# An MLP's first strip groups: rectified products written in place, a weight sum moved to GpSimd, and the last output block in two pieces

## The chip, the cores and the metric

The kernel runs on one core of one Trainium2 chip. The metric is the device time of one execution in microseconds (us). Below, PE is TensorE, DVE is VectorE, ACT is ScalarE, POOL is GpSimd and SP is SyncE, which here only issues transfers.

## The reference, cut to what matters

The program is one layer of a flow-matching backbone: attention and DeltaNet branches, an output projection, then an MLP with a squared rectifier. The change touches the MLP alone (D = 1024, FF = 4096; 128 prompt tokens and 512 sample tokens):

```python
def _ffn_sub(x, shift, scale, gate, w_pre, w_post, w1, w2):
    ...
    f = jnp.square(jax.nn.relu(h @ w1)) @ w2
    ...
```

`h` is the normalised and modulated input. The product with `w2` is normalised again, multiplied by a gate and added to `x`.

## The kernel before

**Tiles and precision.** The 640 tokens stand in five tiles of 128: tile 0 is the prompt, tiles 1 to 4 the sample. Every matrix product is made from three: each operand is split into a high part (`whi`, `mhi`, a cast on ACT) and the rest (`wlo`, `mlo`, a subtraction on DVE or POOL), and high by high, low by high and high by low are summed in PSUM. `mm3` (L198, matmuls L202 to L204) and the two `prod` helpers (L1439 to L1441 in `ff1`, L1546 to L1548 in `ff2`) do this. `split` makes the parts of a weight: `whi` in L182, `wlo` in L183. Plain weights are loaded by SP in `load_raw` (L174) into a small pool of buffers.

**Before the MLP.** Per token tile, `x` is normalised: statistics on ACT, `xn` on DVE (L1357), transposes on PE (L1361), scale and shift on DVE (L1366 from PSUM, L1367), then `mhi` on ACT (L1368) and `mlo` on DVE (L1369). Tile 4 comes last and everything that PE does with tiles 3 and 4 waits for its two `mlo`.

**The MLP** goes in eight groups of 512 hidden columns. Group 0 (`ff1_first`, L1404) is a plain product: four blocks `fb` of 128 columns, each over token tiles 0 to 2 and then 3 and 4. Its results, rectified and squared, are four quadrant tiles named c11, c12, c21 and c22 (all called `c` in the profile). `fops` (L1494) splits them and builds their sums (A11, A12, A22, S1 to S4, each with an `h` and an `l` part) for the second product.

Groups 1 to 7 (`ff1(g)`, L1422) take their 2 x 2 blocks of weights and tokens through seven products in place of eight, with sums of weights (S1, S2, S3, and S2 once more after A12 is added to it) and sums of tokens (T0, T1, T2, made on POOL in L1588 and split by ACT and DVE in L1483 to L1487). The products A11 and A12 come first, S2, S3 and S1 next. S2, then S1 and the second S2, are accumulated upon A11's PSUM tiles (`x`, called `ps_mm`), so each waits until `so_far` (L1445, a COPY on ACT) has taken the sum so far into a quadrant tile of the new group. That quadrant tile is the one in which the group before had its c12; what reads that as S1 must be done. `ff2(g)` (L1531) goes in the same way, with weight sums T1 to T3, and adds its products into the result tiles `R`.

**Weight sums.** They live in four shared buffers, the `sm` tag (L1386). S1, S3, T1 and T3 are made by transfers: SP loads the one block (L1395), then a transfer issued by POOL adds the other block onto it (L1396). S2 and T2 are added on POOL (L1389). In `ff1_first` the rectified tiles `rl` (L1416) take turns in the same four buffers.

**Order.** Each engine goes through its instructions in order. The orders are laid out ahead by a scheduler that simulates a timeline, so an edit at one place also moves neighbours.

**The end.** After the last group, five output blocks (None for the prompt, then four of the sample) take the last group's `w2` products, two halves of 512 columns each. Per block: add or subtract into `R` (L1630, L1632), squares with their sums on ACT (L1636), the gate multiply on POOL (L1637), a short chain for the scale (L1638 to L1641), scale and residual on DVE (L1644), and stores from SP (L1646), 64 rows by 512 columns each.

Of the kernel before, what the change touches and what calls it, by code (L numbers as in the profile page):

```python
# [13 lines left out]
AF = mybir.ActivationFunctionType  # L14
ALU = mybir.AluOpType
AX = mybir.AxisListType
# [81 lines left out]
def body(ctx: ExitStack, tc: tile.TileContext, I, O, dbg=None):  # L98
    nc = tc.nc
    dbg = dbg or {}  # L100
    V, S, G, PE = nc.vector, nc.scalar, nc.gpsimd, nc.tensor
# [64 lines left out]
    def load_raw(src, pool=None, tag="raw"):  # L166
        if raw3[0] and tag == "raw":
            raw3[1] += 1
            if raw3[1] % 3 == 0:
                pool, tag = (raw3[0], 1), "raw3"  # L170
        pool = pool or (rawp if tag == "raw" else (wpool, 4))
        raw = pool[0].tile([P, 1024], F32, tag=tag, name="raw", bufs=pool[1])
        with tc.issue_after(behind[0]) if behind else ExitStack():
            lastd[0] = nc.sync.dma_start(raw, src).ins  # L174
        return raw
# [22 lines left out]
    def mm3(out, pairs):  # L198

        n = len(pairs)  # L200
        for i, (ah, al, bh, bl) in enumerate(pairs):
            PE.matmul(out, ah, bh, start=(i == 0), stop=False)  # L202
            PE.matmul(out, ah, bl, start=False, stop=False)  # L203
            PE.matmul(out, al, bh, start=False, stop=(i == n - 1))  # L204
# [104 lines left out]
    with tc.tile_pool(name="xp", bufs=1, side="right") as xp:  # L309
# [7 lines left out]
        with tc.manual_schedule(engines={mybir.EngineType.SP}):  # L317
# [4 lines left out]
            for a, b in ((0, 2), (2, 4), (4, 5)):  # L322
                for t in range(a, b):
                    for i in range(2):
                        sq = xp.tile([P, 512], F32, tag="xsq", name="xsq", bufs=2)
# [5 lines left out]
                for t in range(a, b):  # L331
                    for i in range(2):
                        V.tensor_scalar(xh[i][:, t], xh[i][:, t], rr[:, t - a : t - a + 1], None, op0=ALU.mult)
                        ps = ps_t3()
# [1051 lines left out]
    def sm(name, a=None, b=None):  # L1386
        x = fa.tile([P, 1024], F32, tag="sm", name=name, bufs=4)
        if a is not None:
            G.tensor_tensor(x, a, b, op=ALU.add)  # L1389
        return x  # L1390

    def sm_dram(name, a, b):

        x = sm(name)
        nc.sync.dma_start(x, a)  # L1395
        nc.gpsimd.dma_start(x, b, accum_op=ALU.add)  # L1396
        return x
# [6 lines left out]
    def ff1_first():  # L1404
        c = f_tiles()
        w = {q: load_w(I["w_ff1"][0, i], 4, 256) for q, i in (((0, 0), 0), ((1, 0), 3), ((0, 1), 1), ((1, 1), 2))}
        for t0, t1 in TG:
            for fb in range(4):
                wd = (t1 - t0) * 128
                fs = slice(fb % 2 * 128, fb % 2 * 128 + 128)  # L1410
                ps = ps_ff(fb)
                mm3(by_tile(ps[:, :wd]), [(w[kh, fb // 2][0][:, k, fs], w[kh, fb // 2][1][:, k, fs],
                                           mhi[:, t0:t1, 4 * kh + k], mlo[:, t0:t1, 4 * kh + k])
                                          for kh in range(2) for k in range(4)])
                rl = sm("rl")
                S.activation(rl[:, :wd], ps[:, :wd], AF.Relu)  # L1416
                for th in range(2):
                    r = rl[:, :wd].rearrange("p (t h c) -> p t h c", h=2, c=64)[:, :, th]
                    V.tensor_tensor(c[fb // 2, th][:, fb % 2].rearrange("p (t c) -> p t c", c=64)[:, t0:t1], r, r, op=ALU.mult)
        return c  # L1420

    def ff1(g):  # L1422

        W11, W21, W22, W12 = [I["w_ff1"][g, i] for i in range(4)]
        A11, A12 = load_raw(W11), load_raw(W12)
        S1, S3 = sm_dram("S1", W21, W22), sm_dram("S3", W21, W11)
        A22 = load_raw(W22)
        c = f_tiles()
        x = [ps_ff(s)[:, :320] for s in range(2)]

        def prod(raw, B, ps, first=True):

            hi, lo = split(raw, 4, 256)
            for s in range(2):
                fs = slice(s * 128, s * 128 + 128)
                for k in range(4):
                    bh, bl = [t[:, k] if len(t.shape) == 3 else t[:, :, k] for t in B]
                    o = ps[s] if len(bh.shape) == 2 else ps[s].rearrange("p (t c) -> p t c", c=64)
                    PE.matmul(o, hi[:, k, fs], bh, start=(first and k == 0), stop=False, skip_group_check=not first)  # L1439
                    PE.matmul(o, hi[:, k, fs], bl, start=False, stop=False, skip_group_check=not first)  # L1440
                    PE.matmul(o, lo[:, k, fs], bh, start=False, stop=(k == 3), skip_group_check=not first)  # L1441

        def so_far(out, ps):
            for s in range(2):
                S.copy(out[:, s], ps[s])  # L1445

        def add(out, a, ps):
            for s in range(2):
                V.tensor_tensor(out[:, s], a[:, s], ps[s], op=ALU.add)

        def done(out, op=ALU.min):
            V.scalar_tensor_tensor(out, out, 0.0, out, op0=op, op1=ALU.mult)

        B11, B12, B21, B22 = [[quad(t, *q) for t in (mhi, mlo)] for q in ((0, 0), (0, 1), (1, 0), (1, 1))]
        prod(A11, B11, x)
        so_far(c[0, 1], x)
        y = [ps_ff(2 + s)[:, :320] for s in range(2)]
        prod(A12, B21, y)
        add(c[0, 0], c[0, 1], y)
        done(c[0, 0], ALU.max)  # L1460
        S2 = sm("S2", S1, A11)
        prod(S2, TT[1], x, False)
        so_far(c[1, 0], x)
        y = [ps_ff(2 + s)[:, :320] for s in range(2)]
        prod(S3, TT[2], y)
        prod(S1, TT[0], x, False)
        so_far(c[1, 1], x)
        add(c[1, 1], c[1, 1], y)
        done(c[1, 1])
        G.tensor_tensor(S2, A12, S2, op=ALU.add)  # L1470
        prod(S2, B22, x, False)
        for s in range(2):
            S.activation(c[0, 1][:, s], x[s], AF.Relu)
        S.activation(c[0, 1], c[0, 1], AF.Square)
        prod(A22, B12, y, False)
        add(c[1, 0], c[1, 0], y)
        done(c[1, 0])
        return c
# [130 lines left out]
    with tc.tile_pool(name="fin", bufs=2, side="right", reuse_waits="tile") as fin_:  # L1609
        gB2 = gate_bcast(1, fin_)  # L1610
        w = {(kh, nh): split(w2_raw(7, kh, nh), 2, 512) for nh in range(2) for kh in range(2)}
        for blk in (None, (0, 0), (1, 0), (0, 1), (1, 1)):
            r = 0 if blk is None else 1
            if blk is None:
                parts = [(slice(0, 128), 0, slice(0, 128))]
                y = [R[4][:, n] for n in range(2)]
                lhs = [[x[:, k] for x in fpr] for k in range(4)]
            else:
                th, pair = blk
                parts = [(slice(64 * j, 64 * j + 64), 1 + 2 * pair + j, slice(64 * th, 64 * th + 64)) for j in range(2)]  # L1620
                y = [R[2 * th + n][:, pair] for n in range(2)]
                lhs = [[x[:, k, 64 + 128 * pair : 192 + 128 * pair] for x in fq[fh, th]] for fh in range(2) for k in range(2)]
            x1 = fin_.tile([P, D], F32, tag="x1", name="x1")
            for ps_, t, cs in parts:
                nc.scalar.dma_start(x1[ps_], x1_d[t, cs])
            for n in range(2):
                ps = ps_t3()
                mm3(ps, [(*lhs[2 * i + k], w[i, n][0][:, k], w[i, n][1][:, k]) for i in range(2) for k in range(2)])
                if blk is not None and n == 1:
                    V.tensor_tensor(y[n], ps, y[n], op=ALU.subtract)  # L1630
                else:
                    V.tensor_tensor(y[n], y[n], ps, op=ALU.add)  # L1632
            sq = fin_.tile([P, D], F32, tag="xn", name="fsq2")
            s1 = fin_.tile([P, 8], F32, tag="fs1", name="fs1")
            for i in range(2):
                S.activation(sq[:, i * 512 : i * 512 + 512], y[i], AF.Square, accum_out=s1[:, i : i + 1])  # L1636
                G.tensor_tensor(y[i], y[i], gB2[:, r, i * 512 : i * 512 + 512], op=ALU.mult)  # L1637
            V.tensor_tensor(s1[:, 2:3], s1[:, 0:1], s1[:, 1:2], op=ALU.add)  # L1638
            V.tensor_scalar(s1[:, 2:3], s1[:, 2:3], 1.0 / D, EPS, op0=ALU.mult, op1=ALU.add)
            S.activation(s1[:, 3:4], s1[:, 2:3], AF.Sqrt)  # L1640
            V.reciprocal(s1[:, 4:5], s1[:, 3:4])  # L1641
            for i in range(2):
                sl = slice(i * 512, i * 512 + 512)
                V.scalar_tensor_tensor(y[i], y[i], s1[:, 4:5], x1[:, sl], op0=ALU.mult, op1=ALU.add)  # L1644
                for ps_, t, cs in parts:
                    nc.sync.dma_start(O["y"][t, cs, sl], y[i][ps_])  # L1646
    lctx.close()


# [94 lines left out]
```

## Time and profile before

| what | value |
|---|---|
| median of three runs | 1165.41 us (1163.5, 1165.41, 1168.72) |
| profiled execution, its time | 1168.25 us |
| profiled execution, its span | 1166.5 us |
| mean granted PE clock | 0.974 |
| traffic | 176.39 MB, mean 151 GB/s |

The span runs from the first to the last event in the trace, and the times in the views count from its start. A row of a timeline has start, duration, engine, line, operation, output and inputs; in brackets stands how long the engine was idle before it and what released it. In windows, the clock is the share of full speed that was granted to PE. The chain of waits follows the work that ended last back from the end, at each step to what released it.

### The profile page before, as it was taken

The numbers are of one execution on the slowest core, as the hardware profiler recorded it, in microseconds if no ns is written. First come the engines' busy times: TensorE is split into PE (matmuls) and PEld (weight loads), VectorE is DVE, ScalarE is ACT, GpSimd is POOL, SyncE is SP. The second block draws the span as 40 slices with busy tenths as digits, with TensorE's granted clock in tenths as the row PEclk, the third lists the DMA queues.
The fourth block names the chain that finished last, engine by engine and source line by source line (L and its number), as shares of the span: only waits on it lengthen the run. The fifth ranks groups of instructions, "written<-read, shape, count | busy, mean of one in ns | idle before, by whom it ended". The sixth has DMA issues, their size and how long they took to land.

```text
span 1166.5 us, 25002 instructions
## 1 busy us (share of the span) xinstructions
PE 1086.5 (93%) x10016; PEld 957.6 (82%) x10016; DVE 871.7 (75%) x1686; ACT 525.1 (45%) x1138; POOL 321.6 (28%) x247
## 2 busy tenths in 40 slices
PE   4999999989899999978999999989999999999996
PEld 3779999878777778867776999988979898897975
DVE  6567897596777685594655767888797989889785
ACT  5435352526444444423346353455444444444532
POOL 1343302100000000121221505544353535435213
PEclk9998999999989999988999999989999999999998
DMA  8831014546645544736233572066655555666515
GB/s 298 312 127 44 23 41 172 187 148 211 202 157 185 161 148 140 211 95 198 87 104 122 198 253 109 19 170 173 178 144 134 141 165 158 165 169 150 169 37 145
DMA packets 75061, 176.39 MB, mean 151 GB/s; under 512 B 16952, under 2 KB 31048, under 8 KB 74944
## 3 DMA queue, kind: packets, MB, share of 16 engines
q1 hardware_dynamic: 57136, 134.60, 34.5%
q0 software_dynamic: 4928, 15.08, 7.6%
q10 hardware_dynamic: 12880, 25.10, 6.8%
q8 instruction: 79, 1.29, 0.5%
q14 instruction: 38, 0.31, 0.1%
HBM read 150.63 MB, written 24.12 MB: 150 GB/s over the span
## 4 chain that ended last, share of the span: by engine, by line
PE 69%; DVE 18%; DMA 4%; ACT 4%; issue 3%; SPq 1%; POOL 0%; ACTq 0%; DVEq 0%; POOLq 0%
PE ps_mm L968 5%; PE ps_mm L969 4%; PE ps_mm L970 4%; DVE wlo L183 4%; PE ps_mm L202 3%; PE ps_mm L203 3%; PE ps_mm L204 3%; PE ps_mm L1441 3%; PE ps_mm L1439 3%; PE ps_mm L1440 3%; DVE R L1529 2%; DVE y L523 2%; PE ps_st L1440 2%; PE ps_st L1439 2%; PE ps_st L1441 2%
## 5 line engine op out<-in xcount | busy, mean ns | idle before, releaser
L968 PE MATMUL ps_mm<-hhi,whi 128*128 128x320 f32 x384 | 132.4, 345 | 12.5 <-ACT gth L947 8.7
L970 PE MATMUL ps_mm<-hhi,wlo 128*128 128x320 f32 x384 | 123.5, 322 | 2.0 <-DVE wlo L934 2.0
L969 PE MATMUL ps_mm<-hlo,whi 128*128 128x320 f32 x384 | 123.5, 322 | 0.0
L183 DVE TENSOR_TENSOR wlo<-raw,whi 128x1024 fp32r<-128x1024 f32 x66 | 87.6, 1335 | 41.6 <-ACT whi L182 41.2
L182 ACT CAST whi<-raw 128x1024 fp32r<-128x1024 f32 x89 | 92.3, 1046 | 37.0 <-PE ps_mm L1440 10.3
L968 PEld LDWEIGHTS ps_mm<-hhi,whi 128*128 128x128 f32 x384 | 76.8, 200 | 26.2 <-ACT gth L947 13.1
L1224 POOL TENSOR_SCALAR bias<-bias 128x256 f32<-128x256 f32 x24 | 21.5, 899 | 221.6 <-DMA bias<-in_bias_dram 213.8
L183 POOL TENSOR_TENSOR wlo<-raw,whi 128x1024 fp32r<-128x1024 f32 x23 | 56.4, 2456 | 82.0 <-ACT whi L182 82.0
L970 PEld LDWEIGHTS ps_mm<-hhi,wlo 128*128 128x128 f32 x384 | 76.8, 200 | 2.2 <-DVE wlo L934 2.2
L969 PEld LDWEIGHTS ps_mm<-hlo,whi 128*128 128x128 f32 x384 | 76.8, 200 | 0.1
L183 DVE TENSOR_TENSOR wlo<-S,whi 128x1024 fp32r<-128x1024 f32 x28 | 57.3, 2068 | 7.4 <-ACT whi L182 7.4
L202 PE MATMUL ps_mm<-hhi,whi 128*128 128x320 f32 x192 | 61.1, 318 | 0.0
L203 PE MATMUL ps_mm<-hlo,whi 128*128 128x320 f32 x192 | 60.6, 316 | 0.0
L204 PE MATMUL ps_mm<-hhi,wlo 128*128 128x320 f32 x192 | 60.2, 313 | 0.0
L183 DVE TENSOR_TENSOR wlo<-T,whi 128x1024 fp32r<-128x1024 f32 x28 | 44.0, 1570 | 16.8 <-ACT whi L182 16.8
L659 POOL DMA_DIRECT2D rls<-ai_d x10 | 5.1, 510 | 181.7 <-PE ps_tb L622 168.2
L934 DVE TENSOR_TENSOR wlo<-raw,whi 128x1024 fp32r<-128x1024 f32 x28 | 34.3, 1229 | 25.2 <-ACT whi L930 24.9
L182 ACT CAST whi<-T 128x1024 fp32r<-128x1024 f32 x28 | 29.4, 1050 | 34.2 <-PE ps_mm L1440 17.2
L523 DVE SCALAR_TENSOR_TENSOR y<-cvb,cw,y 128x644 f32<-128x644 f32 x48 | 42.6, 887 | 0.9
L947 ACT ACTIVATE gth<-ps_mm 128x320 f32<-128x320 f32 x32 | 13.9, 437 | 64.5 <-PE ps_mm L970 42.8
L182 ACT CAST whi<-S 128x1024 fp32r<-128x1024 f32 x28 | 28.6, 1050 | 29.8 <-PE ps_tb L204 12.4
L202 PEld LDWEIGHTS ps_mm<-hhi,whi 128*128 128x128 f32 x192 | 36.8, 192 | 0.7 <-ACT cvb L519 0.3
(559 smaller groups left out, 3599.0 us busy)
## 6 DMA issues: line engine op xcount, KB each, us to landing
raw<-in_w_ff_dram SPq DMA_DIRECT2D x57, 512.0 KB
raw<-in_w_ada_dram SPq DMA_DIRECT2D x48, 512.0 KB
raw<-in_w_gate_dram SPq DMA_DIRECT2D x16, 512.0 KB
S<-in_w_ff_dram SPq DMA_DIRECT2D x14, 512.0 KB
T<-in_w_ff_dram SPq DMA_DIRECT2D x14, 512.0 KB
S<-in_w_ff_dram POOLq DMA_DIRECT2D x14, 512.0 KB, 5.6
T<-in_w_ff_dram POOLq DMA_DIRECT2D x14, 512.0 KB, 6.8
raw<-in_w_dn_dram SPq DMA_DIRECT2D x12, 512.0 KB
```

The source lines that it names most:

```text
L182: S.copy(hi, raw)
L183: eng.tensor_tensor(lo, raw, hi.bitcast(F32), op=ALU.subtract)
L202: PE.matmul(out, ah, bh, start=(i == 0), stop=False)
L203: PE.matmul(out, ah, bl, start=False, stop=False)
L204: PE.matmul(out, al, bh, start=False, stop=(i == n - 1))
L523: V.scalar_tensor_tensor(y, b[:, j : j + 644], cw[:, mt * 5 + j : mt * 5 + j + 1], y, op0=ALU.mult, op1=ALU.add)
L968: PE.matmul(ps, ah, bh, start=(k == 0), stop=False)
L969: PE.matmul(ps, ah, bl, start=False, stop=False)
L970: PE.matmul(ps, al, bh, start=False, stop=(k == KT - 1))
L1439: PE.matmul(o, hi[:, k, fs], bh, start=(first and k == 0), stop=False, skip_group_check=not first)
L1440: PE.matmul(o, hi[:, k, fs], bl, start=False, stop=False, skip_group_check=not first)
L1441: PE.matmul(o, lo[:, k, fs], bh, start=False, stop=(k == 3), skip_group_check=not first)
```

## The change

Three edits. In `ff1_first` the rectifier no longer writes one `rl` tile per block but the two halves of the quadrant tiles themselves, and the squares are made in place. For group 1, A21 is loaded plainly as A22 is, and S1 is their sum on POOL; the other groups keep the transfers. In the last output block, the second half is made in two pieces of 256 columns; the gate multiplies of these are on DVE; the sum of the squares' sums is a reduction (in every block); and the stores of its second 64 rows are issued by ACT.

```diff
@@ ff1_first
-                rl = sm("rl")
-                S.activation(rl[:, :wd], ps[:, :wd], AF.Relu)
                 for th in range(2):
-                    r = rl[:, :wd].rearrange("p (t h c) -> p t h c", h=2, c=64)[:, :, th]
-                    V.tensor_tensor(c[fb // 2, th][:, fb % 2].rearrange("p (t c) -> p t c", c=64)[:, t0:t1], r, r, op=ALU.mult)
+                    r = c[fb // 2, th][:, fb % 2].rearrange("p (t c) -> p t c", c=64)[:, t0:t1]
+                    S.activation(r, ps[:, :wd].rearrange("p (t h c) -> p t h c", h=2, c=64)[:, :, th], AF.Relu)
+                    V.tensor_tensor(r, r, r, op=ALU.mult)
...
@@ ff1
-        S1, S3 = sm_dram("S1", W21, W22), sm_dram("S3", W21, W11)
-        A22 = load_raw(W22)
+        if g == 1:
+
+            A21, A22 = load_raw(W21), load_raw(W22)
+            S1, S3 = sm("S1", A21, A22), sm_dram("S3", W21, W11)
+        else:
+            S1, S3 = sm_dram("S1", W21, W22), sm_dram("S3", W21, W11)
+            A22 = load_raw(W22)
...
@@ the output blocks
-                mm3(ps, [(*lhs[2 * i + k], w[i, n][0][:, k], w[i, n][1][:, k]) for i in range(2) for k in range(2)])
-                if blk is not None and n == 1:
-                    V.tensor_tensor(y[n], ps, y[n], op=ALU.subtract)
-                else:
-                    V.tensor_tensor(y[n], y[n], ps, op=ALU.add)
+
+                pieces = [slice(0, 256), slice(256, 512)] if (blk, n) == ((1, 1), 1) else [slice(0, 512)]
+                for cs in pieces:
+                    mm3(ps[:, cs], [(*lhs[2 * i + k], w[i, n][0][:, k, cs], w[i, n][1][:, k, cs]) for i in range(2) for k in range(2)])
+                    if blk is not None and n == 1:
+                        V.tensor_tensor(y[n][:, cs], ps[:, cs], y[n][:, cs], op=ALU.subtract)
+                    else:
+                        V.tensor_tensor(y[n][:, cs], y[n][:, cs], ps[:, cs], op=ALU.add)
...
-            for i in range(2):
-                S.activation(sq[:, i * 512 : i * 512 + 512], y[i], AF.Square, accum_out=s1[:, i : i + 1])
-                G.tensor_tensor(y[i], y[i], gB2[:, r, i * 512 : i * 512 + 512], op=ALU.mult)
-            V.tensor_tensor(s1[:, 2:3], s1[:, 0:1], s1[:, 1:2], op=ALU.add)
+            last = blk == (1, 1)
+            cols = [(0, 512), (512, 768), (768, 1024)] if last else [(0, 512), (512, 1024)]
+            for i, (a, b) in enumerate(cols):
+                yi = y[a // 512][:, a % 512 : a % 512 + b - a]
+                S.activation(sq[:, a:b], yi, AF.Square, accum_out=s1[:, 5 + i : 6 + i])
+                (V if i and last else G).tensor_tensor(yi, yi, gB2[:, r, a:b], op=ALU.mult)
+            V.tensor_reduce(s1[:, 2:3], s1[:, 5 : 5 + len(cols)], axis=AX.X, op=ALU.add)
...
-                for ps_, t, cs in parts:
-                    nc.sync.dma_start(O["y"][t, cs, sl], y[i][ps_])
+                for j, (ps_, t, cs) in enumerate(parts):
+                    (nc.scalar if j and last else nc.sync).dma_start(O["y"][t, cs, sl], y[i][ps_])
```

The lines below `ff1_first` move on by four, so L1588 of before is L1592, L1445 is L1449 and L1487 is L1491; in the output blocks the squares are L1646 and the scaling is L1654.

The first place is POOL, from its last preparations of tile 3 to the weight sums of group 1. `S` with a number is a sum in an `sm` buffer (before: S_9859 is S1, S_9862 is S3, S_9936 is S2). Before:

```order
L1588 TENSOR_TENSOR h2f<-h2f 128x4x64
L1487 TENSOR_TENSOR mlo<-h2f,mhi 128x4x64 x3
L1588 TENSOR_TENSOR h2f<-h2f 128x4x64 x4
L1487 TENSOR_TENSOR mlo<-h2f,mhi 128x4x64
L1396 DMA S_9859<-in_w_ff_dram 128x1024
L1396 DMA S_9862<-in_w_ff_dram 128x1024
L1389 TENSOR_TENSOR S_9936<-S_9859,raw 128x1024
```

With the change (S_9863 is S1, S_9937 is S2, S_9865 is S3):

```order
L1592 TENSOR_TENSOR h2f<-h2f 128x4x64
L1389 TENSOR_TENSOR S_9863<-raw 128x1024
L1491 TENSOR_TENSOR mlo<-h2f,mhi 128x4x64 x3
L1389 TENSOR_TENSOR S_9937<-S_9863,raw 128x1024
L1396 DMA S_9865<-in_w_ff_dram 128x1024
L1592 TENSOR_TENSOR h2f<-h2f 128x4x64
L1396 DMA T_10100<-in_w_ff_dram 128x1024
```

The sums S1 and S2 now stand ahead of and behind the three `mlo`, and S2 no longer stands behind two accumulating transfers.

The second place is DVE, from the first of tile 4's two L1367 additions to the second of its two L1369 subtractions. Before:

```order
L1367 TENSOR_TENSOR h2f<-h2f,mod_76 128x512
L1419 TENSOR_TENSOR c_9484<-rl 128x192
L1419 TENSOR_TENSOR c_9485<-rl 128x192
L1367 TENSOR_TENSOR h2f<-h2f,mod_76 128x512
L1369 TENSOR_TENSOR mlo<-h2f,mhi 128x512
L1419 TENSOR_TENSOR c_9484<-rl 128x192
```

With the change:

```order
L1367 TENSOR_TENSOR h2f<-h2f,mod_76 128x512
L1418 TENSOR_TENSOR c_9484<-c_9484 128x192
L1418 TENSOR_TENSOR c_9485<-c_9485 128x192
L1418 TENSOR_TENSOR c_9486<-c_9486 128x192
L1367 TENSOR_TENSOR h2f<-h2f,mod_76 128x512
L1418 TENSOR_TENSOR c_9487<-c_9487 128x192
L1418 TENSOR_TENSOR c_9486<-c_9486 128x192
L1418 TENSOR_TENSOR c_9487<-c_9487 128x192
L1369 TENSOR_TENSOR mlo<-h2f,mhi 128x512
```

Six squares of tiles 0 to 2 stand ahead of the first `mlo` of tile 4, where two stood.

The third place is DVE again, around S1l, the last reader of the tile that the COPY (L1445, now L1449) writes over. Before:

```order
L1487 TENSOR_TENSOR S3l<-c_9484,S3h 128x512
L1487 TENSOR_TENSOR S1l<-c_9485,S1h 128x512
L1511 TENSOR_TENSOR c_9484<-c_9487,c_9484 128x2x256
L1514 TENSOR_TENSOR c_9486<-c_9484,c_9486 128x2x256
L1484 SCALAR_TENSOR_TENSOR S2l<-c_9484,S2h 128x512
L1487 TENSOR_TENSOR S4l<-c_9486,S4h 128x512
L1449 TENSOR_TENSOR c_9867<-c_9868,ps_st_9903 128x320
L1449 TENSOR_TENSOR c_9867<-c_9868,ps_st_9904 128x320
L1452 SCALAR_TENSOR_TENSOR c_9867<-c_9867 128x640
L183 TENSOR_TENSOR wlo<-S_9936,whi 128x1024
L183 TENSOR_TENSOR wlo<-S_9862,whi 128x1024
L183 TENSOR_TENSOR wlo<-S_9859,whi 128x1024
```

With the change (the rows `wlo<-S_9937`, of S2, and `wlo<-S_9865`, of S3, stand some lines ahead of this piece):

```order
L1491 TENSOR_TENSOR S3l<-c_9484,S3h 128x512
L1512 TENSOR_TENSOR c_9485<-c_9487,c_9485 128x2x256
L1515 TENSOR_TENSOR c_9484<-c_9487,c_9484 128x2x256
L183 TENSOR_TENSOR wlo<-S_9863,whi 128x1024
L1491 TENSOR_TENSOR A12l<-c_9486,A12h 128x512
L1491 TENSOR_TENSOR A22l<-c_9487,A22h 128x512
L1491 TENSOR_TENSOR S1l<-c_9485,S1h 128x512
L1488 SCALAR_TENSOR_TENSOR S2l<-c_9484,S2h 128x512
L1518 TENSOR_TENSOR c_9486<-c_9484,c_9486 128x2x256
L183 TENSOR_TENSOR wlo<-S_9937,whi 128x1024
```

The three `wlo` of the sums, which followed S1l, now precede it.

## The prediction

> **What bounds the kernel now.** I read the page's busy shares first, then windows over the groups of the MLP, then the chain of waits where these windows leave time unused.
>
> ```profile
> span 1166.5 us, 25002 instructions
> PE 1086.5 (93%) x10016; PEld 957.6 (82%) x10016; DVE 871.7 (75%) x1686; ACT 525.1 (45%) x1138; POOL 321.6 (28%) x247
> ...
> 763.60:817.40 53.80, 48.23 (x262) 44.15 (x261) 44.38 (x49) 29.48 (x48) 24.82 (x17) 0.94 0.69 179
> ...
> 868.90:920.50 51.60, 50.19 (x278) 44.47 (x277) 45.41 (x51) 24.13 (x36) 23.52 (x15) 1.00 0.58 155
> ```
>
> The windows' columns are length, then busy time of PE, weight load, DVE, ACT and POOL, then granted clock and DMA. A later group (868.9 to 920.5) keeps PE busy 50.19 of 51.60 us: PE bounds the groups, and whatever PE loses ahead of them arrives at the end of the kernel. The first strip group (763.6 to 817.4) is longer and has a clock of 0.94. Finer windows show where that comes from:
>
> ```profile
> 745.00:750.00 5.00, 5.00 (x34) 4.84 (x32) 3.80 (x8) 2.42 (x7) 1.46 (x2) 1.00 0.20 79
> 750.00:755.00 5.00, 3.45 (x24) 2.85 (x24) 5.00 (x9) 2.81 (x8) 2.89 (x4) 1.00 0.00 0
> ...
> 770.00:775.00 5.00, 0.83 (x6) 0.57 (x4) 2.87 (x5) 0.53 (x1) 2.06 (x1) 0.97 0.85 169
> 775.00:780.00 5.00, 3.60 (x13) 3.60 (x14) 3.62 (x3) 3.14 (x4) 3.39 (x3) 0.50 0.77 167
> 780.00:785.00 5.00, 5.00 (x31) 5.00 (x31) 5.00 (x3) 2.75 (x4) 3.83 (x3) 0.85 0.74 252
> ```
>
> There are two holes: a small one at 750 to 755 (PE 3.45 busy, clock stays 1.00), and a large one at 770 to 776, after which the clock is 0.50 and then 0.85. The chain of waits and the timelines of PE, POOL, ACT and SP say what ends the large one:
>
> ```profile
> 771.17 0.89 DVE c L1449 x2
> 772.08 0.84 DVE c L1452
> 772.96 2.32 POOL S L1389
> 775.30 1.05 ACT whi L182
> 776.40 0.63 PE ps_mm L1439
> ...
> 784.38 0.29 PE ps_st L1441 x2
> ```
> ```profile
> 776.40 0.63 PE L1439 MATMUL ps_mm<-T2h,whi 128*128 128x320 f32 x1 [5.57 <-ACT whi L182]
> ```
> ```profile
> 678.20 13.99 SPq L174 DMA_DIRECT2D raw<-in_w_ff_dram  x9
> ...
> 760.60 2.34 SPq L1395 DMA_DIRECT2D S<-in_w_ff_dram  x2
> 765.77 0.95 POOL L1396 DMA_DIRECT2D S<-in_w_ff_dram  x1 [2.13 <-DMA S<-in_w_ff_dram]
> 768.63 0.75 ACT L1445 COPY c<-ps_mm 128x320 f32<-128x320 f32 x2 [1.24 <-DVE S1l L1487]
> ```
>
> The two weight sums S1 and S3 are first loaded at 760.60, when rectified tiles give their slots back; S1's second operand is accumulated by a transfer issued at 765.77. Then POOL adds S2 at 772.96 (2.32 us), ACT splits it, and PE's S2 product starts at 776.40 after 5.57 us of waiting. At a clock near 0.5 until about 781.5, its matmuls run at half rate: 13 start in 776.40 to 780, about 0.27 apart, where two take 0.29 later at full rate (784.38). The 19 matmuls to 781.6 would take 2.8 us at full clock; the product's **full-clock start** is therefore 781.6 − 2.8 = 778.8. The A12 product ahead of it ends at about 770.7. So gap and slow clock together hold **8.1 us**, and that is all the head can give.
>
> **The change, edit by edit.** *In-place rectification.* Eight relus become sixteen of half the width. ACT's two 320-column copies out of PSUM take 0.75 (row 768.63), so I put eight at 0.4 and sixteen at 0.25 to 0.3: 1 to 2 us more on ACT, which is busy 2.42 and 2.81 of 5 us in the rows of 745 to 755. It delays nobody by itself. It frees the slots, so the S3 and T1 loads no longer wait for 760.6; they are at worst as late as now.
>
> *S1 on GpSimd.* One 512 KB transfer goes, and the sum needs only plain loads, which stand in SP's queue far ahead (nine weight loads are issued by 692, row 678.20). The add now sits on POOL directly behind the L1588 subtraction, and the S2 add behind POOL's three mlo. What stands beside them on DVE is tile 4's normalisation, on which PE waits:
>
> ```profile
> 743.26 1.18 POOL L1588 TENSOR_TENSOR h2f<-h2f 128x256 f32<-128x256 f32 x1
> 748.54 2.83 POOL L1487 TENSOR_TENSOR mlo<-h2f,mhi 128x256 fp32r<-128x256 f32 x3 [4.09 <-ACT mhi L1486]
> ...
> 755.96 3.88 POOL L1588 TENSOR_TENSOR h2f<-h2f 128x256 f32<-128x256 f32 x2 [1.77 <-DVE mlo L1369]
> ...
> 782.18 2.42 POOL L1389 TENSOR_TENSOR T<-raw,T 128x1024 f32<-128x1024 f32 x1 [1.17 <-DVE wlo L183]
> ```
> ```profile
> 745.74 0.75 DVE L1357 TENSOR_SCALAR xn<-x,s 128x1024 f32<-128x1024 f32 x1
> 748.48 0.68 DVE L1367 TENSOR_TENSOR h2f<-h2f,mod 128x512 f32<-128x512 f32 x1
> 749.07 1.70 DVE L1419 TENSOR_TENSOR c<-rl 128x192 f32<-128x192 f32 x2
> 750.70 1.21 DVE L1367 TENSOR_TENSOR h2f<-h2f,mod 128x512 f32<-128x512 f32 x1
> 751.83 0.68 DVE L1369 TENSOR_TENSOR mlo<-h2f,mhi 128x512 fp32r<-128x512 f32 x1
> 752.44 2.78 DVE L1419 TENSOR_TENSOR c<-rl 128x192 f32<-128x192 f32 x6
> ...
> 757.22 1.22 DVE L183 TENSOR_TENSOR wlo<-raw,whi 128x1024 fp32r<-128x1024 f32 x1
> 765.45 0.68 DVE L1487 TENSOR_TENSOR A12l<-c,A12h 128x512 fp32r<-128x512 f32 x1
> ...
> 782.22 3.46 DVE L183 TENSOR_TENSOR wlo<-S,whi 128x1024 fp32r<-128x1024 f32 x1
> ```
> ```profile
> 752.57 0.39 PE L203 MATMUL ps_mm<-mlo,whi 128*128 128x256 f32 x1 [1.06 <-DVE mlo L1369]
> ```
>
> These rows show DVE and POOL **taking turns**: the same wlo subtraction takes 1.22 us alone and 3.46 when a POOL add of 2.42 us starts 0.04 ahead of it; the L1367 add takes 0.68 alone and 1.21 beside POOL's three mlo, and two squares there take 1.70 where six take 2.78 otherwise. I take SBUF-only operations of the two engines as exclusive, first come first served. By these durations, and the changed order, tile 4's chain becomes:
> - POOL's S1 add: 744.44 to 746.9 (2.33 and starting time). xn, ready at 745.74, starts behind it and ends at 747.7, not 746.5: +1.2.
> - The transposes and three h2f operations, 0.6 each, end at 749.8, not 749.1.
> - Three squares, each behind one of POOL's mlo (about 1.0 a turn): to 752.8.
> - The S2 add asks at 752.6 and runs 2.2 to 2.4 us; the second L1367 waits for it and ends at 755.6, not 751.9.
> - Three further squares stand ahead of the first mlo, at 0.26 each with their waits; mlo (0.60) ends at 757.0, not 752.5: **+4.5**.
>
> PE then idles about 5.4 us from 751.6, the A12 product ends near 774.9, not 770.7, and 4.2 of the 8.1 us is gone. The bound on the good side is a POOL that costs DVE nothing: the old 752.6 and 770.7. With a partial slowing of both engines the first mlo is some 2 us late.
>
> *The new wait at S2.* S2 accumulates in the PSUM tiles of the A11 product, so it waits for the COPY of L1445 (0.75 us), which overwrites a tile whose last reader is S1l on DVE (row 768.63). Before, that hid ahead of the S2 sum. In the new order S1l stands behind three wlo of S. From tile 4's first mlo to S1l are 33 DVE instructions: at 1.2 for each of five wlo, 0.6 for each 512-wide one, 0.2 to 0.35 for the small ones, 16.2 us if alone; I add 5.8 us for turns with four L1588 subtractions, one mlo and the S2 + A12 sum (2.8) of POOL. S1l ends at 756.4 + 16.2 + 5.8 = 778.4 to 778.6, the first COPY 0.4 later: S2's product starts at **779.0**. Against the full-clock start 778.8 that is +0.2: the old wait goes and this one ends at the same time. If POOL cost nothing, S2 would start at 771.6 (−7.2); if DVE could keep POOL out for as long as it has work, at 783.0 (+4.2). The partial slowing gives 776.9.
>
> *Clock.* The gap of 5.6 us was followed by 6.8 us at half clock, the hole of 750 to 753 by none. A further slow window of 3.4 us costs at most 1.7 us. Two gaps of 5.4 and 4.1 us lie between these cases: 0 to 3.4, and I take 1.7, nearer to the longer gap for one of them.
> The Trainium skill, "TensorE: Matmul & The Clock Gate", section "Why this matters for your kernels", warns of idle gaps over about 3 us, after which the clock drops. The rows at 0.50 and at 1.00 fit it. Read strictly it charges both new gaps, and the sum would be 1.7 us higher than mine.
>
> *Tail.* The timelines of DVE, ACT, POOL and SP and the windows at the end:
>
> ```profile
> 1157.60 0.69 DVE L1630 TENSOR_TENSOR R<-ps_tp,R 128x512 f32<-128x512 f32 x1 [0.78 <-PE ps_tp L204]
> 1159.95 1.65 DVE L1644 SCALAR_TENSOR_TENSOR R<-R,fs,x 128x512 f32<-128x512 f32 x2
> ```
> ```profile
> 1158.33 0.63 ACT L1636 ACTIVATE fsq<-R 128x512 f32<-128x512 f32 x1 [2.02 <-DVE R L1630]
> ```
> ```profile
> 1159.12 1.26 POOL L1637 TENSOR_TENSOR R<-R,gB 128x512 f32<-128x512 f32 x1 [1.16 <-ACT fsq L1636]
> ```
> ```profile
> 1156.18 7.17 SPq L1646 DMA_DIRECT2D out_y_dram<-R  x8
> ```
> ```profile
> 1162.00:1164.00 2.00, 0.00 (x0) 0.00 (x0) 0.00 (x0) 0.00 (x0) 0.00 (x0) 0.50 0.88 195
> ```
>
> Matmul time stays: 24 of half the width. Subtract and square of the last 256 columns cost about 0.42 each, not 0.69 and 0.63: −0.4. POOL's multiply no longer runs beside the first L1644 (two take 1.65, so 0.96 and 0.69): −0.3. The gate multiply on DVE (about 0.4) lies beside the square. So the first store starts 0.7 earlier. SP issued the last four stores from about 1160.95, when the first L1644 is done, to 1163.35, 0.6 each; two queues end that about 1.2 us sooner still, but the transfers run at DMA 0.88 at 1162 to 1164, so most of that is hidden. Tail: **−1.0**, from 0 (landing bound by something unseen) to −2.0 (both savings).
> The Trainium skill, "DMA: Bandwidth & Descriptors", section "Issuing engines are not separate DMA queues", says that several issuers save only issuing time, on the same DMA engines. By it the queues give nothing and the tail is −0.7; the 0.88 agrees.
>
> **The sum.** +0.2 (wait exchanged) + 1.7 (clock) − 1.0 (tail) = +0.9 on the profiled execution (span 1166.5, time 1168.25): 1169.1. That execution is 2.8 above the median of 1165.41, so against the median **1166.3**.
>
> **The rivals.**
> - *The head works as meant:* POOL's adds cost DVE little, S2 starts at 771.6 without a slow window. −7.2 − 1.0 = −8.2: 1157.2. For it: the loads are early, and POOL is idle 4 us at 744 to 748. Against it: 3.46 against 1.22.
> - *It works by half:* both engines slow down without excluding each other, S2 at 776.9, one slow window: −1.9 + 1.7 − 1.0 = −1.2: 1164.2. It also covers a change that only shifts its wait.
> - *Slower:* DVE passes POOL whenever it has an instruction ready, so the S2 add waits, whi follows late, and S2's product starts at 783.0. +4.2, two slow windows (+3.4), −1.0: +6.6, 1172.0. It decides once S2 starts after about 782. For it: the two L1588 in the row of 755.96 took 3.88, the one at 743.26 only 1.18, while DVE ran on beside them. Against it: the three mlo at 748.54 got their turns, at DVE's cost.
>
> **How the numbers follow.** Chances: forecast 0.50, by half 0.20, as meant 0.18, slower 0.12. The measurement can tell about 0.5%, 5.8 us, from no change: 1159.6 to 1171.2. Faster takes the case as meant (0.18); slower takes the slow case and 0.01 of the forecast (0.13); the rest is within (0.69). The forecast's own range is 1162.5 to 1169.5. The range 1157.0 to 1171.5 leaves out less than half of each outer case and a few hundredths for scatter of the runs (1163.5 to 1168.72).
>
> **What would show it.** Right: POOL's S1 add at 744 to 747 beside a lengthened xn; PE idle some 5 us at 752 to 757 and again 4 us ahead of S2, released by the COPY on ACT, with clock 0.5 behind; S2 near 779. Wrong: tile 4's mlo before 754, or PE going from A12 into S2 without a wait; wrong too if S2 waits for whi, not for the COPY. In the tail, PE's end to the span's end should fall from 8.9 to about 7.9.

## The result, and the profile after

The changed kernel took a median of 1169.49 us in 16 runs (1163.91 to 1172.55), the kernel before 1163.42 us in 16 runs beside it. The ratio is 1.0041, 95% interval 1.0022 to 1.0060: **4.8 us slower** (2.6 to 7.0). That is also the difference of the two means; the medians differ by 6.1. The profiled execution has a span of 1168.2 us, 1.7 above before's.

Single executions of one kernel differ by several microseconds ahead of the MLP already, so the profiles are compared from a fixed point of the program: the **mark**, the start of tile 4's statistics on DVE (L1354, at 745.11 before and 743.85 after). From it I count the *head*, up to the square root of the last-but-one output block, and the *last part*, from there to the end of the span. Before: 409.3 and 12.1. After: 411.4 and 13.0.

Windows after, with columns as in the prediction (the program stands 1.26 us earlier here than before, by the two marks):

```profile
745.00:750.00 5.00, 4.15 (x28) 3.75 (x27) 4.25 (x6) 2.47 (x8) 2.42 (x3) 1.00 0.86 285
750.00:755.00 5.00, 0.67 (x4) 0.27 (x2) 5.00 (x7) 1.33 (x5) 4.49 (x4) 0.76 0.06 25
755.00:760.00 5.00, 4.40 (x22) 4.40 (x23) 4.91 (x8) 0.87 (x4) 3.58 (x5) 0.56 0.99 161
...
775.00:780.00 5.00, 0.69 (x5) 0.43 (x4) 5.00 (x9) 3.36 (x6) 1.63 (x2) 0.99 0.63 211
780.00:785.00 5.00, 5.00 (x25) 5.00 (x25) 5.00 (x6) 1.08 (x3) 3.85 (x1) 0.67 0.90 208
785.00:790.00 5.00, 5.00 (x36) 5.00 (x35) 2.08 (x4) 2.62 (x4) 0.87 (x1) 1.00 0.53 86
```

PE is nearly idle twice, at 750 to 755 (0.67 of 5 us) and at 775 to 780 (0.69), and both times the clock is low behind it: 0.76 and 0.56, then 0.67. Before, there was one such hole. PE's timeline names what ends them (the last two fields: idle time, and what released it):

```profile
746.38 0.66 PE L1361 MATMUL ps_tb<-cst,xn 128*128 128x128 f32 x4 [0.85 <-DVE xn L1357]
755.60 0.58 PE L203 MATMUL ps_mm<-mlo,whi 128*128 128x256 f32 x1 [4.66 <-DVE mlo L1369]
779.76 0.51 PE L1443 MATMUL ps_mm<-T2h,whi 128*128 128x320 f32 x1 [4.30 <-ACT c L1449]
...
1158.07 0.38 PE L202 MATMUL ps_tp<-whi,f 128*128 128x256 f32 x1 [1.03 <-DVE R L1637]
```

The first wait is for tile 4's `mlo` on DVE, the second for the COPY, the third is new to the last output block. POOL's and DVE's timelines show the way to the first:

```profile
743.14 2.63 POOL L1389 TENSOR_TENSOR S<-raw 128x1024 f32<-128x1024 f32 x1
748.35 2.83 POOL L1491 TENSOR_TENSOR mlo<-h2f,mhi 128x256 fp32r<-128x256 f32 x3 [2.58 <-ACT mhi L1490]
751.14 2.45 POOL L1389 TENSOR_TENSOR S<-S,raw 128x1024 f32<-128x1024 f32 x1
```
```profile
744.47 1.85 DVE L1357 TENSOR_SCALAR xn<-x,s 128x1024 f32<-128x1024 f32 x1
...
748.88 2.51 DVE L1418 TENSOR_TENSOR c<-c 128x192 f32<-128x192 f32 x3
751.32 2.82 DVE L1367 TENSOR_TENSOR h2f<-h2f,mod 128x512 f32<-128x512 f32 x1
754.06 0.88 DVE L1418 TENSOR_TENSOR c<-c 128x192 f32<-128x192 f32 x3
754.87 0.68 DVE L1369 TENSOR_TENSOR mlo<-h2f,mhi 128x512 fp32r<-128x512 f32 x1
...
778.56 0.68 DVE L1491 TENSOR_TENSOR S1l<-c,S1h 128x512 fp32r<-128x512 f32 x1
```

`xn` (0.75 us before) takes 1.85 beside the S1 add and ends within 0.6 us of it. Three squares take 2.51 beside POOL's three `mlo`, and three others 0.88 with POOL idle or issuing. The L1367 addition starts to wait at 751.32 and takes 2.82 beside the S2 add of 2.45. The last row is S1l, whose end at 779.24 releases the COPY.

### The profile page after: what moved, and what is told of

It reads as the page before. It is cut to its first block, busy times and chain, and to the rows that moved or that the text cites. A ratio compares the mean times of both kernels' runs of the same rounds, so it can differ in the third digit from the quotient of the medians.

```text
span 1168.2 us, 25043 instructions
## 1 busy us (share of the span) xinstructions
PE 1088.9 (93%) x10028; PEld 960.2 (82%) x10028; DVE 875.3 (75%) x1689; ACT 525.9 (45%) x1148; POOL 321.8 (28%) x246
## 5 line engine op out<-in xcount | busy, mean ns | idle before, releaser
L968 PEld LDWEIGHTS ps_mm<-hhi,whi 128*128 128x128 f32 x384 | 77.1, 201 | 25.0 <-ACT gth L947 11.9
L183 DVE TENSOR_TENSOR wlo<-S,whi 128x1024 fp32r<-128x1024 f32 x28 | 53.5, 1927 | 2.9 <-ACT whi L182 2.9
```

The costliest lines, as they stand in the source:

```text
L183: eng.tensor_tensor(lo, raw, hi.bitcast(F32), op=ALU.subtract)
L968: PE.matmul(ps, ah, bh, start=(k == 0), stop=False)
```

## The experiments

Each part of the change was put in alone or taken out, and then each suspected wait was moved. The table has the profiled execution of each; S2 is the start of PE's S2 product behind the mark, "first" and "second" are PE's waits for tile 4's `mlo` and ahead of S2, all from the timelines and waits of PE. The two runs with before's head beside before itself (e2, e5) show how much the head scatters: 408.4 to 410.8.

| run | what | first | second | S2 | head | last part | ratio (95%) |
|---|---|---|---|---|---|---|---|
| before | | 1.1 | 5.6 | 31.3 | 409.3 | 12.1 | |
| after | the change | 4.7 | 4.3 | 35.9 | 411.4 | 13.0 | 1.0041 (1.0022 to 1.0060) |
| e1_head | without the last block's edit | 4.7 | 4.3 | 36.7 | 415.4 | 12.2 | 1.0021 (0.9997 to 1.0045) |
| e2_tail | the last block's edit alone | 1.1 | 6.7 | 32.4 | 410.8 | 12.4 | 0.9993 (0.9970 to 1.0016) |
| e3_inplace | in-place rectifier alone | 2.5 | 4.9 | 33.1 | 410.5 | 12.2 | 1.0008 (0.9985 to 1.0031) |
| e4_s1add | S1 on GpSimd alone | 1.1 | 4.0 | 29.7 | 408.7 | 12.1 | 1.0000 (0.9978 to 1.0022) |
| e5_banks | e2, pieces in two PSUM tiles | 1.1 | 6.2 | 32.0 | 408.4 | 11.1 | 0.9976 (0.9958 to 0.9993) |
| e7_s1l | e1, S1l ahead of the wlo | 4.7 | none | 31.3 | 414.2 | 12.2 | 1.0045 (1.0004 to 1.0086) |
| e8_late | e1, adds behind tile 4 | 2.5 | 7.2 | 35.4 | 412.6 | 12.3 | 1.0035 (1.0011 to 1.0059) |
| e9_both | e7 and e8 | 2.5 | 2.2 | 30.4 | 409.5 | 12.2 | 0.9992 (0.9967 to 1.0016) |
| e10_dve | e4 and e5, adds on DVE | 1.1 | 7.3 | 33.1 | 411.9 | 11.5 | 1.0009 (0.9982 to 1.0035) |
| e11_comb | e4 and e5 | 1.1 | 4.1 | 29.5 | 408.1 | 11.1 | **0.9971** (0.9946 to 0.9996) |
| e13_copy | e10, COPY first on ACT | 1.1 | 1.7 | 28.9 | 408.3 | 11.2 | 0.9974 (0.9946 to 1.0003) |
| e14_mended | the change, with e5's tiles | 4.7 | 4.3 | 36.6 | 413.1 | 11.7 | 1.0030 (1.0002 to 1.0057) |

**e1_head: the change without its edit of the last block.** The output blocks are those of before; everything else is the change.

> The rectifier in place and S1 on GpSimd, with the output blocks of before. Theory (DVE and GpSimd take turns, then the COPY waits for S1l): PE waits about 4.7 us for tile 4's mlo and 4.3 us for the COPY, each followed by a clock of 0.5; between tile 4's statistics and the start of the last output block +2.1 us against before, and the end as before (15.7 us); ratio 1.002. Rival (the loss is all in the end): 0 up to the last block, ratio 1.000.

Both waits came as in the change, to 0.01 us (4.67 and 4.29). The head was 415.4, more than expected: 6.1 above before, where after is 2.1 above. So most of the loss lies in the head, but its size differs between executions of one order. The last part was 12.2, as expected. The timing of this run alone is not clear of no change (0.9997 to 1.0045).

**e2_tail: the last block's edit alone.** The lines of the change from `pieces` on, put on the kernel before.

> Only the last output block's edits, on the kernel of before. Theory (the second piece's matmuls wait until DVE has read the first piece out of the same PSUM tile): PE waits 1.0 us inside the last block, which ends 0.8 us later than before; nothing changes ahead of it; ratio 1.001. Rival (as the prediction had it): no wait, the last block ends 1.0 us sooner, ratio 0.999.

PE's wait was there (1.0 us), and the square root of the last-but-one block to PE's end was 4.47 us, as in after, against 3.17 before. What follows PE was 1.0 us shorter (7.95 against 8.92), so the last part lost only 0.3, not 0.8. The ratio cannot tell it from 1. The rival's end without a wait is out.

**e3_inplace: the rectifier in place, nothing else.**

```diff
-                rl = sm("rl")
-                S.activation(rl[:, :wd], ps[:, :wd], AF.Relu)
...
+                    V.tensor_tensor(r, r, r, op=ALU.mult)
```

> Only the rectifier in place; S1 is made by transfers as before. Theory: without S1's add xn is not held up; the first wait of PE (tile 4's mlo) is 1.5 to 3 us, from three squares more and GpSimd's mlo; the wait for the COPY stays, since the three wlo still precede S1l, at 3 to 4 us; up to the last block -1 to -2 us against before, ratio 0.999. Rival (the exclusion of DVE and GpSimd is not what costs): both waits are as long as with the whole change, +2 us.

The first wait was 2.51 us. By its length against before (1.1) and after (4.7), the squares that the scheduler puts ahead of `mlo` cost 1.4 us and the two adds on POOL the other 2.2; e8_late tests the latter. The second wait was 4.87 us and ended with the COPY, as forecast:

```profile
750.65 0.39 PE L203 MATMUL ps_mm<-mlo,whi 128*128 128x256 f32 x1 [2.51 <-DVE mlo L1369]
775.19 0.64 PE L1438 MATMUL ps_mm<-T2h,whi 128*128 128x320 f32 x1 [4.87 <-ACT c L1444]
```

So the in-place rectifier alone exchanges one wait for another; the head of 410.5 (expected 1 to 2 below before) shows no gain.

**e4_s1add: S1 on GpSimd, nothing else.** Since the rectified tiles keep the shared buffers, both adds now come after tile 4.

```diff
+            A21, A22 = load_raw(W21), load_raw(W22)
+            S1, S3 = sm("S1", A21, A22), sm_dram("S3", W21, W11)
```

> Only S1 on GpSimd from plain loads; the rectified tiles stay in the shared buffers, so both adds come after tile 4 is done. Theory: no first wait beyond before's 1.1 us; S1 and S2 are added at about 763.5 to 769, S2's whi and the COPY are ready by 771 to 773, PE waits 1 to 3 us instead of 5.6 and the clock stays up; up to the last block -4 to -6 us, ratio 0.995 to 0.996. Rival (the sums cost DVE as much here as they gain): within 1 us of before.

There was no longer first wait, and S2 started 1.6 us sooner than before (29.7 against 31.3), but the second wait was 4.0, not 1 to 3, and the clock fell behind it as before. The timelines of POOL, DVE, ACT and PE say why:

```profile
767.45 2.61 POOL L1389 TENSOR_TENSOR S<-raw 128x1024 f32<-128x1024 f32 x1
770.14 2.74 POOL L1389 TENSOR_TENSOR S<-S,raw 128x1024 f32<-128x1024 f32 x1
```
```profile
767.69 2.92 DVE L1492 TENSOR_TENSOR A11l<-c,A11h 128x512 fp32r<-128x512 f32 x1
770.53 2.70 DVE L1419 TENSOR_TENSOR c<-rl 128x128 f32<-128x128 f32 x2
773.15 0.68 DVE L1512 TENSOR_TENSOR c<-c,c 128x512 f32<-128x512 f32 x1
```
```profile
776.93 0.75 ACT L1450 COPY c<-ps_mm 128x320 f32<-128x320 f32 x2 [1.25 <-DVE S1l L1492]
777.57 1.06 ACT L182 CAST whi<-S 128x1024 fp32r<-128x1024 f32 x1
```
```profile
778.68 0.63 PE L1444 MATMUL ps_mm<-T2h,whi 128*128 128x320 f32 x1 [4.00 <-ACT whi L182]
```

Two DVE steps that take 0.68 and 0.48 alone take 2.92 and 2.70 beside the two adds; that is 4.5 us on the way to S1l and to the COPY. On ACT the `whi` of S2, for which PE waits, stands right behind the COPY. The head gained 0.5, the timing nothing measurable. The rival was right on the sum.

**e5_banks: the last block's edit with a PSUM tile for each piece.**

```diff
-                ps = ps_t3()
...
                 for cs in pieces:
+                    ps = ps_t3()
```

> As e2_tail, but the two pieces of the last half are made in PSUM tiles of their own. Theory (the shared PSUM tile makes PE wait): the wait of 1.0 us is gone, PE's last matmul comes 3.2 us after the last-but-one block's square root as before (4.5 with the shared tile), the end 8 to 8.5 us behind PE, so the last block ends 0.5 to 1.0 us sooner than before. Rival (the half-width matmuls themselves cost the time): still 4.5 us.

PE has no wait in the last block, and the last part is 11.1 us: 0.95 less than before, 1.3 and 1.9 less than with the shared tile (e2 and after). The ratio is 0.9976 (0.9958 to 0.9993), so this kernel is faster than the one before, by 2.8 us (0.8 to 4.9). The last part accounts for 0.95 of these; the order of the head is that of before, and where the rest comes from is not shown.

**e7_s1l: the wlo of the sums placed behind S1l on DVE** (on e1_head).

```diff
+            with tc.issue_after(f["S1i"].ins) if g == 1 and all(raw is not z for z in (A11, A12, A22)) else ExitStack():
-            hi, lo = split(raw, 4, 256)
+                hi, lo = split(raw, 4, 256)
```

> As e1_head, but DVE's three wlo of S2, S3 and S1 are placed behind S1l; GpSimd's adds stay. Theory: the first wait (4.7 us for mlo) stays, the second shrinks from 4.3 to about 1 us, now for wlo of S2, and the clock stays up behind it; up to the last block 3 to 5 us less than e1_head and after (head 407 to 409, 409.3 before). Rival (the COPY's wait is not the limit, the sums are): the second wait stays above 3 us.

The wait ahead of S2 went, as expected. S2 started at 31.3, as in the kernel before. The head fell only by 1.2 from e1_head's: at 784.9, in a product of `ff2`, PE waited 3.3 us for a `whi` on ACT. By the chain of waits, this stood behind steps of DVE and ACT that began with the `whi` of the sum S2 + A12, which POOL added late:

```profile
773.66 5.68 POOL L1475 TENSOR_TENSOR S<-raw,S 128x1024 f32<-128x1024 f32 x1 [6.08 <-DVE wlo L183]
```
```profile
772.37 3.49 DVE L183 TENSOR_TENSOR wlo<-S,whi 128x1024 fp32r<-128x1024 f32 x3
775.78 0.68 DVE L1519 TENSOR_TENSOR c<-c,c 128x512 f32<-128x512 f32 x1
```

The add takes 2.66 us in e10_dve; here 5.68, since DVE first went on with its own steps, two whole `wlo` and at least one more. Read as turns, POOL and DVE exclude each other here too, but not in the order of asking. The expected head of 407 to 409 was a miss: the wait moved on.

**e8_late: GpSimd's adds placed behind its last subtraction for tile 4** (on e1_head).

```diff
-            S1, S3 = sm("S1", A21, A22), sm_dram("S3", W21, W11)
+            with tc.issue_after(t4.ins):
+                S1 = sm("S1", A21, A22)
+            S3 = sm_dram("S3", W21, W11)
```

> As e1_head, but GpSimd's S1 and S2 adds are placed behind its last subtraction for tile 4; the wlo stay ahead of S1l. Theory (turns of DVE and GpSimd in front of tile 4's mlo cost the first wait): xn takes 0.75 us again, the first wait falls from 4.7 to about 2.5 us as in e3_inplace, A11 starts 20 to 21.5 us behind the statistics (24.4 to 25.2 with early adds); the wait for the COPY stays at 4 to 5 us; head 409 to 411. Rival (the squares in place cost the first wait): it stays above 4 us.

`xn` took 0.75 us, L1367 0.68, the first wait 2.51 and A11 started 21.0 us behind the mark, all as expected. This shows that the adds made the difference from 2.5 to 4.7. The wait for the COPY was 7.2, not 4 to 5, because the adds now met DVE further on:

```profile
753.47 2.63 POOL L1389 TENSOR_TENSOR S<-raw 128x1024 f32<-128x1024 f32 x1
756.74 2.72 POOL L1389 TENSOR_TENSOR S<-S,raw 128x1024 f32<-128x1024 f32 x1
```
```profile
754.06 3.13 DVE L183 TENSOR_TENSOR wlo<-raw,whi 128x1024 fp32r<-128x1024 f32 x1 [0.26 <-ACT whi L182]
757.11 2.70 DVE L1418 TENSOR_TENSOR c<-c 128x128 f32<-128x128 f32 x2
...
766.54 4.71 DVE L183 TENSOR_TENSOR wlo<-S,whi 128x1024 fp32r<-128x1024 f32 x1 [0.21 <-ACT whi L182]
```

The last row is a third collision, with POOL's `mlo` and the sum S2 + A12 (767.52, 2.64 us). So S1l ended 34.9 us behind the mark, hardly sooner than after (35.4), while PE came to its wait 3.4 us sooner.

**e9_both: e7_s1l and e8_late together** (both edits as above).

> e7_s1l and e8_late together. Theory: first wait about 2.5 us, second 0.5 to 2 us, S2's product starts 29 to 31 us behind the statistics at full clock (31.3 and half clock before); head 405 to 407, ratio 0.996 to 0.998. Rival (PE is held by DVE's sum of work whatever the order): head within 1 us of before's 409.3.

The waits fell to 2.5 and 2.2 us and S2 started at 30.4, as the theory said, and the clock stayed up behind S2. The head, however, was 409.5, not 405 to 407: smaller waits for `wlo` (2.6 us in three) and for the next COPY followed. The rival's number came out. Against e1_head, which differs by these two edits alone, the head is 5.9 shorter, and the ratio is 0.9992: with both waits cut, the loss of the head is gone.

**e10_dve: the adds of S1 and S2 on DVE** (on e4_s1add, with e5's last block).

```diff
-            S1, S3 = sm("S1", A21, A22), sm_dram("S3", W21, W11)
+            S1, S3 = sm("S1", A21, A22, V), sm_dram("S3", W21, W11)
...
-        S2 = sm("S2", S1, A11)
+        S2 = sm("S2", S1, A11, V if g == 1 else G)
```

> As e4_s1add (rectified tiles in the shared buffers, S1 from plain loads), but DVE makes the S1 and S2 adds of group 1 itself, and the end as in e5_banks. Theory (GpSimd's adds cost because DVE must take turns with them): each add is 1.2 us in DVE's own queue instead of 2.2 to 2.6 us of its waiting; S1l ends about 27 us behind the statistics, S2's product starts at 27.5 (29.7 in e4_s1add) after a wait of about 2 us, with no slow clock behind it; group 1 is done at 48 to 51 us (53.3 to 54.2 before), the head is 404 to 407 and the last block 1 us shorter; ratio 0.994 to 0.997. Rival (DVE's queue is the limit, whoever adds): S2 at 29.5 or later, ratio 0.998 to 1.000.

Each add took 1.21 us on DVE, and S1l ended at 772.1, 26.8 us behind the mark: the DVE part of the theory held. S2 started at 33.1 all the same. ACT's and PE's timelines:

```profile
776.00 1.99 ACT L182 CAST whi<-S 128x1024 fp32r<-128x1024 f32 x2 [6.14 <-DMA S<-in_w_ff_dram]
777.90 0.74 ACT L1450 COPY c<-ps_mm 128x320 f32<-128x320 f32 x2
```
```profile
778.37 0.63 PE L1444 MATMUL ps_mm<-T2h,whi 128*128 128x320 f32 x1 [7.34 <-ACT c L1450]
```

The tile that the COPY writes over was free at 772.1, but in ACT's order two `whi` stand ahead of it, the first of S3, whose accumulating transfer was issued at 767.0 and landed at 776.

**e13_copy: the splits of S3 and S1 behind the COPY on ACT, and behind the addition of the A12 product on DVE** (on e10_dve).

```diff
+                if g == 1 and any(raw is z for z in late):
+                    ex.enter_context(tc.issue_after(cp.ins))
+                    ex.enter_context(tc.issue_after(ad.ins))
+                    ex.enter_context(tc.issue_after(f["S4h"].ins))
```

> As e10_dve, but on ACT the splits of S3 and S1 stand behind the COPY and the last token sum, and on DVE behind the addition of A12's product. Theory (in e10_dve the COPY was ready at 27 us behind the statistics and only queued on ACT behind whi of S3, whose transfers landed at 31): S2's product starts at 27 to 28 after a wait of about 2 us, with the clock up; S3's transfers are the next limit, a second wait of 1 to 3 us; group 1 done at 48 to 51, head 404 to 407, ratio 0.994 to 0.996. Rival (something else holds the COPY): S2 above 30.

The waits had the size expected: 1.7 us ahead of S2 and 1.5 us at S3. The second was ended by DVE, though, not by S3's transfer: a step there took 3.30 us beside POOL's sum S2 + A12 (769.72, 2.71 us), and the addition that frees the PSUM tile came behind it.

```profile
769.69 3.30 DVE L1498 SCALAR_TENSOR_TENSOR S2l<-c,S2h 128x512 fp32r<-128x512 f32 x1
```
```profile
774.13 0.39 PE L1449 MATMUL ps_st<-T1h,whi 128*128 128x320 f32 x1 [1.50 <-DVE c L1462]
```

Moreover, A11 started 1.5 us later than in e10_dve, behind a slow clock that followed the short hole at tile 4's `mlo`, and S2 so at 28.9, not 27 to 28; the clock fell once more behind the second pair of waits. The head was 408.3 (404 to 407 expected) and the ratio 0.9974, not clear of 1.

**e11_comb: e4_s1add's head with e5_banks' last block.**

> The head of e4_s1add and the end of e5_banks. Theory: the two parts add up, head 408 to 410, the last block 11.1 to 11.5 us (12.1 before); ratio 0.997 to 0.999. Rival: no difference from before, 1.000.

Head 408.1, last part 11.1, ratio 0.9971 (0.9946 to 0.9996): this is the lowest ratio that was measured, 3.4 us below before (0.5 to 6.3), and it differs from the change by keeping `rl` in the shared buffers and by one PSUM tile.

**e14_mended: the change, with a PSUM tile for each piece.**

> The whole change, with the two pieces of the last half in PSUM tiles of their own. Theory: the head as in after and e1_head (411 to 415), the last block 11.1 to 11.5 us (13.0 with the change as it is), so 1.5 us less than after; ratio 1.001 to 1.003. Rival (the end is not additive to the head): as after, 1.004.

Head 413.1, last part 11.7 (11.1 to 11.5 expected), ratio 1.0030: 1.3 us of the last part came back; the head's loss stayed.

## Why the prediction was right, and where a term was off

The forecast was no difference beyond 0.5%, at 1166.3 us in a range from 1157.0 to 1171.5; measured were 0.41% and 1169.49 us. The waits and what ends them came as forecast, the size of the loss did not, and that the time fits is in part luck. The forecast stands on the median of three runs, 1165.41; the 16 runs of the same kernel have 1163.42, and these 2 us hid as much of the miss. The change itself, 4.8 us (2.6 to 7.0), leaves out the forecast's 0.9. Both terms that make up the forecast's sum, clock and tail, were taken too favourably. Step by step, counted from the mark:

- **Turns of DVE and POOL ahead of tile 4: right, and shown.** The prediction's chain has `xn` ending at 2.6, the second L1367 at 10.5 and `mlo` at 11.9; the profile after has 2.5, 10.3 and 11.7. e8_late takes the adds away from there and `xn` falls back to 0.75 us and the wait from 4.7 to 2.5. e3_inplace gives the same 2.5; 1.1 of it was there before, and the rest is the share of the squares.
- **The new wait at S2: right, and shown.** Forecast 4.1 us, ended by the COPY behind S1l; measured 4.30, so ended. e7_s1l moves S1l ahead of the three `wlo` and that wait is gone.
- **The clock: right in kind, too small.** I took 1.7 us. The A12 product ended 31.6 us behind the mark (779.76 − 4.30 − 743.85), 1.8 later than the forecast 29.8, though PE had its `mlo` on time: the clock is at 0.56 in the window of 755. Behind S2, the window at 0.67 holds another 5 × 0.33 = 1.65. Together this is 3.5. By S2's full-clock start the head is 35.9 + 1.65 − 33.7 = 3.9 us later than before, not 1.9. The prediction had set 3.4 beside its own value, by the strict reading of the rule in the Trainium skill, "TensorE: Matmul & The Clock Gate", section "Why this matters for your kernels", on idle gaps over about 3 us. That value came out; as a limit, 3 us did not hold here, since waits of 2.5 us were followed by half clock in three runs (last section).
- **How the slow clock reached S2: overlooked.** S2 did not wait for A12 but for S1l, which ended at 35.4, not 33.3 to 33.5. DVE's own time from tile 4's first `mlo` to S1l was 21.6 us, close to the forecast's 22.0. But DVE stood idle for 2.8 us in between, of which the forecast has nothing, and 2.6 of them were waits for two `whi`, each of which ACT made only when a matmul was done:

```profile
760.21 1.05 ACT L182 CAST whi<-raw 128x1024 fp32r<-128x1024 f32 x1 [3.25 <-PE ps_mm L203]
763.39 1.05 ACT L182 CAST whi<-raw 128x1024 fp32r<-128x1024 f32 x1 [0.73 <-PE ps_mm L203]
```
```profile
761.29 1.23 DVE L183 TENSOR_TENSOR wlo<-raw,whi 128x1024 fp32r<-128x1024 f32 x1 [1.38 <-ACT whi L182]
764.47 1.23 DVE L183 TENSOR_TENSOR wlo<-raw,whi 128x1024 fp32r<-128x1024 f32 x1 [1.22 <-ACT whi L182]
```

PE's matmuls ran at half clock until 759.4, so the delay seems to have passed from PE over ACT to DVE. No run takes the slow clock alone away, so this link is argued from the rows and not shown.

- **How much of it reaches the end.** The three profiles with the change's head have 411.4, 415.4 and 413.1, the three with before's 409.3, 410.8 and 408.4: the means differ by 3.8, the two groups by no overlap but only 0.6 at the closest. Between after and e1_head, which have the same head, 4.0 us lie. In the 60 us behind the mark the mean clock is 0.91 in after and 0.89 in e1_head (0.94 before), and the slow stretches there last 10.2 and 13.7 us; the 3.4 more, at half clock, cost up to 1.7 us. e1_head also has a wait of 1.2 us for a `wlo` at the start of group 2 that after does not have. The rest was not settled.
- **The last block: the step that failed.** "Matmul time stays" and the sum of −1.0 overlooked that both pieces lie in one PSUM tile: the second piece's matmuls waited until DVE had subtracted the first (row 1158.07), and DVE came to that only after the two scalings of the block before. The last part became 0.9 longer in after and 0.3 in e2_tail. With a tile for each piece it became 0.95 shorter (e5_banks). The wait was the missing term.
- **Behind PE: the sum held in some runs, its terms did not.** PE's end to the span's end went from 8.9 to 8.5 in after, not to 7.9, and to 7.9 or 8.0 in e2, e5, e11 and e13 (8.3 in e10, 8.5 in e14). The first scaling ended only 0.38 sooner behind PE's end (2.99 against 3.37, in every run with the edit), not 0.7. The prediction laid DVE's gate multiply beside the square; in after it waited for the square and stood ahead of the reduction, which adds 0.34 us:

```profile
1160.22 0.42 ACT L1646 ACTIVATE fsq<-R 128x256 f32<-128x256 f32 x1 [1.65 <-DVE R L1637]
```
```profile
1160.76 0.43 DVE L1647 TENSOR_TENSOR R<-R,gB 128x256 f32<-128x256 f32 x1 [0.58 <-ACT fsq L1646]
1161.10 0.15 DVE L1648 TENSOR_REDUCE fs<-fs 128x1 f32<-128x3 f32 x1
```

From the first scaling's end to the end of the span it was 5.5 us in after, as before, and 5.0 or 4.9 in e2 and e5; the forecast had taken 0.3 off for the two queues.

Sum of the runs: head +3.8, last part +0.5 (mean of after and e2_tail, 12.7, against 12.2 in the runs without the edit), 4.3 us; the timing says 4.8. The number lies nearer to the slower rival's +6.6 than to the forecast's +0.9, and S2's start, 35.9, halfway between the forecast's 33.9 and that rival's 37.9. Its mechanism is not the one seen, though: POOL got its S2 add at 751.14, and S2 waited for the COPY, not for a late `whi`. That DVE can pass POOL at all, e7_s1l shows. The rivals in which the head gains are out.

## What to carry to other kernels

Before a sum is moved onto GpSimd, look at what DVE does beside it: in the rows shown here each add of about 2.6 us cost DVE 1.1 to 2.2 us at whatever place it stood, which matters wherever another engine waits for DVE. When a wait is taken away, follow the next releaser in each queue's order (here an ACT COPY behind a `whi`, behind a transfer): three of these experiments (e7_s1l, e8_late, e10_dve) removed a cost as planned, and the next wait in line took most of it or all. When a block is cut into pieces, give each piece a PSUM tile of its own: in one shared tile, the reader of the first piece held up the second by 1.0 us here.

## What the runs showed of the hardware

- Turns between DVE and POOL are not always in the order of asking: in e7_s1l POOL's add took 5.68 us (2.66 in e10_dve) while, by these lengths, at least three DVE steps passed it.
- PE waits of 1.7 and 2.2 us ahead of S2 left the clock up (e13_copy, e9_both), those of 4.0 us or more were followed by a slow stretch in every run, and so were the 2.5 us at tile 4's `mlo` in e3_inplace, e8_late and e9_both. Shorter holes can go either way: before and e13_copy have the same wait of 1.1 us at tile 4, with full clock behind the one and a start of A11 1.5 us later behind the other.
- The granted clock follows a grid of time, so what counts is how a wait falls into it. Around the mark, every slow stretch in the 14 profiles lasts 3.41, 6.83 or 10.24 us, one to three times 3.41. Cut into windows of that length from the start of a slow stretch, 5 us ahead of the mark to 70 behind it, they give 322 windows. Behind all 28 in which PE was busy for at most 0.43 of the time, the next window ran at half clock; behind all 282 in which it was busy for more than 0.66, at full clock; behind the 12 between, it went either way. The wait of 1.1 us at tile 4 fell into a window with PE busy for 2.35 of 3.41 us before, and for 1.97 in e13_copy.
- Two queues for the last four stores: last scaling to the end of the span took 4.9 to 5.05 us in the seven profiles with all stores on SP, and 4.3 (four runs), 4.6, 4.8 and 4.9 in the seven with two. The gain is 0 to 0.8 us. That fits the rule of the Trainium skill, "DMA: Bandwidth & Descriptors", section "Issuing engines are not separate DMA queues", that only issuing time is saved.
